# Two transformer blocks on one core: gate one-hots laid out token by token, mapping with one scratch tile, fetched rows asked for earlier, a share of the query weights' low parts on GpSimd

## Chip, core and metric

The kernel runs on one core of a Trainium2 chip. The engines work side by side and wait for one another through semaphores: TensorE (PE; its weight loads are listed as PEld), VectorE (DVE), ScalarE (ACT), GpSimd (POOL) and SyncE (SP), which issues most of the DMA transfers. The metric is the device time of one execution in microseconds. "The profile" is a summary page of one profiled execution, "the trace" what can be asked of that same execution.

## The reference

Two blocks follow each other on 256 tokens of width 2048, all in float32. The part around the change is the retrieval of experts in the first block:

```python
q = (zc @ peer_wq).reshape(PEER_CHUNK, 8, 2, 128)
s1 = einsum('chd,hkd->chk', q[:, :, 0], k1);  s2 = einsum('chd,hkd->chk', q[:, :, 1], k2)
v1, i1 = top_k(s1, 16);  v2, i2 = top_k(s2, 16)
cand = (v1[..., :, None] + v2[..., None, :])          # 16 x 16 sums per head
top_s, top_pos = top_k(cand, 16)
expert = take_along_axis(i1 * 128 + i2, top_pos)      # one of 16384 experts
gate = softmax(top_s)
act = gelu(einsum('chkd,cd->chk', peer_u[expert], zc))
out = einsum('chk,chkd->cd', gate * act, peer_v[expert])
```

Ahead of it stand a pooling mixer and a gated linear recurrence with their projections, behind it an attention block, a convolution and an MLP.

## The kernel before

Weights stream from HBM in pieces of 512 KB, `[128, 8, 128]` float32. The loop over pieces, `p`, sets the order of everything: each round issues the DMAs ahead, makes the piece's operands, issues its eight products on TensorE, and then calls `tick`, which moves the generators on that do the rest (`tasks` at once, `bg` by priority under a budget of estimated costs, the numbers behind `yield`). So the order on each engine is fixed when the program is built, and an engine never overtakes its own queue. A ring of twelve buffers holds the pieces. The pieces of most projections are split in a high part (`wh`, `hi`, by ScalarE) and a low part (`wl`, `lo`, by VectorE), three pieces ahead; `st["share"]` gives so many eighths of a low part to GpSimd. Pieces of the expert matrices `peer_u` and `peer_v` are "plain": they are used as they are (L188), with the 176 tokens of `zn` (or of the gated hidden tiles `hd`, `hb`) as the moving operand.

The first 80 tokens (`SETS`: 64 and 16) get their experts' rows by fetching; for the other 176 all 16384 experts are computed and weighted by a gate matrix. What matters here, in the order of the program:

1. Query pieces (`peer_wq`). `post_wq` makes the scores, `topk_head` finds the best 16 per half and head on VectorE.
2. Pieces of `peer_u` begin. `token_rows` transposes the fetched tokens into `zt` and copies it to all partitions with POOL's DMA queue.
3. `mapping(t)`, for each half of 128 tokens: the softmax of the gates (its exponential is ScalarE's, L642, with a table load ahead of it), and the translation of the winners into expert rows and columns. That is a comparison with an index row, a product and a reduction over 128x2048 elements, for each of two sides (L671, L675, L678). Then TensorE transposes the result (L682 to L684). After the first half, `entries` sends the row numbers and gates to small tiles by POOL's DMAs (L728, L730), and `fetched` starts: three rows of all partitions in flight (L746), each multiplied with `zt` on VectorE (L756).
4. Ahead of `peer_u` step 16 (two pieces each) the loop calls `need(["map0", "map1"])`, so the transposes of the second half stand on TensorE behind the same 256 products in any case.
5. `build_G`: for each group of four tokens a one-hot of the row (A) and a one-hot of the column times the gate (B); A comes from a comparison (L823) and a copy on ScalarE (L824), B from a comparison (L826) and a product with the gate (L827), all `[128, 512]`. TensorE multiplies them token by token (L800), ScalarE keeps the result (L807), and every four groups a DMA writes it to HBM (`Gd`). There are two A/B buffers. Groups are woven between pieces, one `yield` each.
6. Ahead of step 36 the loop calls `need(["G"])` and issues all groups that are left, with no pieces between them: the closing run. Then `load_G` reads the matrices back, and the `peer_v` pieces begin.

A float32 product appears in the trace as two instructions, and as two weight loads.

Of the kernel before, what the change touches and what calls it, by code (L numbers as in the profile page):

```python
# [46 lines left out]
def kernel(ctx: ExitStack, tc: tile.TileContext, a, out, upto=99):  # L47
# [491 lines left out]
    def begin_peer():  # L539
# [21 lines left out]
        st["it4"] = pb.tile([128, 128, 4], BF16, name="it4")  # L561
        pool.tensor_copy(st["it4"], iota_r[:, :, None].to_broadcast([128, 128, 4]))
# [3 lines left out]
        later(normed(), 0)  # L566

# [59 lines left out]
    def mapping(t):  # L627
# [10 lines left out]
        if t == 0:  # L638
            yield from wait("zt")
# [24 lines left out]
        eqs = []  # L664
        for i in range(2):
            if t == 0:
                eq = pb.tile([128, 8, 16, 16], F32, name="eq", tag=f"gs{i}")
            else:
                eq = st["S"][:, i].rearrange("p h a (k b) -> p h (a k) b", k=8)
            eqs.append(eq)  # L670
            dve.tensor_tensor(eq, ab[:, i, :, :, None].to_broadcast([128, 8, 16, 16]),  # L671
                              iota_r[:, None, None, 0:16].to_broadcast([128, 8, 16, 16]), op=ALU.is_equal)
            F = st["F1"] if i == 0 else st["F2"]
            yield 3.2
            dve.tensor_tensor(eq, eq, F[:, t, :, None, :].to_broadcast([128, 8, 16, 16]), op=ALU.mult)  # L675
            yield 2.2
        for i in range(2):
            dve.tensor_reduce(ab[:, i], eqs[i], axis=AX.X, op=ALU.add)  # L678
            yield 2.2
        yield 0.0  # L680
# [4 lines left out]
        if t == 0:  # L685
            entries(ab.rearrange("p i h k -> p i (h k)"), G.rearrange("p h k -> p (h k)"))
# [31 lines left out]
    def entries(ab, G):  # L718
# [4 lines left out]
        st["idx"], st["gat"], st["hid"] = [], [], []  # L723
        for i, (t0, n) in enumerate(SETS):
            x = pb.tile([128, n], U32, name=f"idx{i}")
            g = pb.tile([128, n], F32, name=f"gat{i}")
            for q in range(128 // n):
                pool.dma_start(x[q * n:(q + 1) * n], e[t0:t0 + n, q * n:(q + 1) * n])  # L728
            for q in range(128 // n):
                pool.dma_start(g[q * n:(q + 1) * n], G[t0:t0 + n, q * n:(q + 1) * n])  # L730
            st["idx"].append(x)
            st["gat"].append(g)
            st["hid"].append(pb.tile([128, n], F32, name=f"hid{i}"))
        st["units"] = fetched()

    def fetched():
# [13 lines left out]
        for u in range(3):  # L750
            fetch(u)
        for u, (_, i, s) in enumerate(units):
# [37 lines left out]
    def build_G():  # L790

        pb = st["pb"]
        it4 = st["it4"]
# [23 lines left out]
        for b in range(ND // 4 + 1):  # L817
            if b < ND // 4:
                row, col = (st["T"][:, i, None, 4 * b:4 * b + 4].to_broadcast([128, 128, 4]) for i in range(2))
                gate = st["TG"][:, None, 4 * b:4 * b + 4].to_broadcast([128, 128, 4])  # L820
                A, B = st["oh"][b % 2]
                one = pb.tile([128, 128, 4], BF16, name="om", bufs=2)
                dve.tensor_tensor(one, row, it4, op=ALU.is_equal)  # L823
                act.activation(A, one, AF.Copy)  # L824
                one = pb.tile([128, 128, 4], BF16, name="om", bufs=2)
                dve.tensor_tensor(one, col, it4, op=ALU.is_equal)  # L826
# [42 lines left out]
    def begin_u():  # L869
        ready.add("u0")  # L870

    def begin_hidden():
# [4 lines left out]
        for i in range(2):  # L877
# [3 lines left out]
            one.append([t[:, n + 512 * k:n + 512 * k + 512].rearrange("p (j t) -> p j t", t=4) for k in range(2)])  # L881
# [536 lines left out]
    for p in range(NP):  # L1418
# [108 lines left out]
```

## Time and profile before

| | |
|---|---|
| median of three runs | 3059.46 us (3058.08 to 3060.64) |
| the profiled execution | 3059.16 us |
| its span, from the first to the last instruction | 3057.2 us |
| TensorE busy | 2992.2 us, 98% |
| VectorE busy | 1931.7 us, 63% |
| ScalarE busy | 1053.5 us, 34% |
| GpSimd busy | 337.7 us, 11% |
| mean granted TensorE clock | 0.990 of full speed |

A row of the timeline gives the start, the duration, engine, line, operation, output and inputs; the number behind "x" counts merged instructions, and brackets hold the idle time ahead and what ended it. Matmul ends are modelled, so that the durations of neighbours overlap; their pace is read from starts.

### The profile page before, as it was taken

Reading aid. Unit: us, or ns where it says so; the run is one execution under the profiler, and the core shown is the slowest. Engines: PE = TensorE matmul, PEld = TensorE weight load, DVE = VectorE, ACT = ScalarE, POOL = GpSimd, SP = SyncE. Lnnn points to the kernel's source line nnn. Section 1 sums busy time; section 2 is a strip of 40 time slices with the busy share of each in tenths; the row PEclk is TensorE's granted clock in tenths of the full one; section 3 lists DMA queues with packets and bytes.
Section 4 is the critical chain, followed back from the end, with each engine's and each line's share of the span. In section 5 each row is a group of like instructions: output and inputs, shape, how many; then the busy total and the mean of one; then the engine's idle time right before and its main releaser. Section 6 shows DMA issues by size and latency. Waiting matters only on the chain.

```text
span 3057.2 us, 46147 instructions
## 1 busy us (share of the span) xinstructions
PE 2992.2 (98%) x18156; PEld 2773.8 (91%) x18156; DVE 1931.7 (63%) x3296; ACT 1053.5 (34%) x1642; POOL 337.7 (11%) x307
## 2 busy tenths in 40 slices
PE   9999979999999999999999999999998999999997
PEld 7888969999999999999999888888887888888886
DVE  8868864454444444444452888987658666666767
ACT  7754212220000000000001667657555444444444
POOL 0100020012222222222111100001501000000001
PEclk9999989999999999999999999999999999999998
DMA  7466677779999999999996555565654666665653
GB/s 248 156 187 192 220 220 241 255 282 414 395 395 395 391 390 392 395 397 393 395 359 192 163 176 173 183 196 174 196 189 138 199 183 189 186 187 185 187 186 124
DMA packets 208904, 773.44 MB, mean 253 GB/s; under 512 B 21568, under 2 KB 44416, under 8 KB 187776
## 3 DMA queue, kind: packets, MB, share of 16 engines
q1 hardware_dynamic: 161424, 588.98, 56.3%
q0 software_dynamic: 23984, 169.31, 14.1%
q10 hardware_dynamic: 23280, 12.20, 1.4%
q8 instruction: 144, 2.36, 0.3%
q14 instruction: 72, 0.59, 0.1%
HBM read 755.25 MB, written 13.63 MB: 251 GB/s over the span
## 4 chain that ended last, share of the span: by engine, by line
PE 83%; DVE 1%; ACT 0%; issue 0%
PE mm L188 38%; PE mm L122 28%; PE mm L123 14%; PE g L800 3%; DVE R L1198 0%; DVE z L1213 0%; PE g L778 0%; DVE Y L1461 0%; DVE R L1462 0%; PE s L246 0%; DVE Y L1194 0%; PE g L1113 0%; PE g L1093 0%; PE s L1122 0%; DVE wl L1371 0%
## 5 line engine op out<-in xcount | busy, mean ns | idle before, releaser
L122 PE MATMUL mm<-z,wh 128*128 128x512 f32 x2816 | 1001.3, 399 | 16.1 <-DVE z L1213 9.9
L1360 ACT ACTIVATE wh<-wx 128x1024 fp32r<-128x1024 f32 (+1 forms) x579 | 609.7, 1055 | 698.2 <-PE mm L122 380.9
L1371 DVE TENSOR_TENSOR wl<-wx,wh 128x1024 fp32r<-128x1024 f32 (+1 forms) x579 | 706.3, 1222 | 187.0 <-ACT wh L1360 185.9
L123 PE MATMUL mm<-z,wl 128*128 128x256 f32 x2816 | 789.4, 280 | 5.2 <-DVE wl L1371 5.2
L122 PEld LDWEIGHTS mm<-z,wh 128*128 128x128 f32 x2816 | 530.9, 189 | 141.8 <-issue 8.9
L188 PE MATMUL mm<-zn,wx 128*128 128x176 f32 x4096 | 634.6, 313 | 0.0
L188 PEld LDWEIGHTS mm<-zn,wx 128*128 128x128 f32 x4096 | 620.1, 191 | 0.1
L123 PEld LDWEIGHTS mm<-z,wl 128*128 128x128 f32 x2816 | 533.5, 189 | 7.3 <-DVE wl L1371 7.0
L905 DVE TENSOR_TENSOR R<-R,mm 128x176 f32<-128x176 f32 x256 | 86.1, 336 | 552.7 <-PE mm L188 552.7
L188 PE MATMUL mm<-hb,wx 128*128 128x176 f32 x2560 | 392.4, 313 | 0.0
L188 PEld LDWEIGHTS mm<-hb,wx 128*128 128x128 f32 x2560 | 384.2, 190 | 0.0
L122 PE MATMUL mm<-f,wh 128*128 128x512 f32 x1024 | 364.3, 399 | 0.0
L123 PE MATMUL mm<-f,wl 128*128 128x256 f32 x1024 | 287.6, 281 | 0.0
L122 PEld LDWEIGHTS mm<-f,wh 128*128 128x128 f32 x1024 | 192.4, 188 | 48.1
L188 PE MATMUL mm<-hd,wx 128*128 128x176 f32 x1536 | 235.2, 313 | 0.0
L188 PEld LDWEIGHTS mm<-hd,wx 128*128 128x128 f32 x1536 | 230.5, 190 | 0.0
L855 ACT ACTIVATE hb<-mm 128x176 f32<-128x176 f32 x80 | 25.4, 318 | 593.4 <-PE mm L188 570.5
L123 PEld LDWEIGHTS mm<-f,wl 128*128 128x128 f32 x1024 | 193.4, 189 | 0.0
L746 POOL DMA_INDIRECT ga<-in_peer_u_rows_dram,idx x80 | 107.5, 1343 | 523.6 <-DVE hid L756 430.0
L756 DVE CUSTOM_DVE_ANT_0 ga<-ga 128x2048 f32<-128x2048 f32 x64 | 146.2, 2284 | 10.3 <-DMA ga<-in_peer_u_rows_dram,idx 10.3
L746 POOL DMA_INDIRECT ga<-in_peer_v_rows_dram,idx x80 | 102.2, 1277 | 413.4 <-DVE ga L764 216.6
L764 DVE SCALAR_TENSOR_TENSOR ga<-ga,hid 128x2048 f32<-128x2048 f32 x63 | 147.8, 2345 | 0.0
(377 smaller groups left out, 2678.8 us busy)
## 6 DMA issues: line engine op xcount, KB each, us to landing
wx<-in_peer_u_dram SPq DMA_DIRECT2D x256, 512.0 KB
wx<-in_peer_v_dram SPq DMA_DIRECT2D x256, 512.0 KB
wx<-in_w_in_dram SPq DMA_DIRECT2D x191, 512.0 KB
wx<-in_w_up_dram SPq DMA_DIRECT2D x128, 512.0 KB
wx<-in_w_down_dram SPq DMA_DIRECT2D x128, 512.0 KB
wx<-in_w_out_dram SPq DMA_DIRECT2D x32, 512.0 KB
wx<-in_peer_wq_dram SPq DMA_DIRECT2D x32, 512.0 KB
wx<-in_w_o_dram SPq DMA_DIRECT2D x32, 512.0 KB
```

The lines of the kernel that those rows point to most:

```text
L122: pe.matmul(ps, w[0][:, k], z[:, zk], start=first, stop=False, skip_group_check=True)
L123: pe.matmul(ps[:, 0], w[1][:, k], z[:, zk, 0], start=False, stop=last, skip_group_check=True)
L188: pe.matmul(ps, w[:, k], rhs(half, k), start=k == 0 and (split or half == 0), stop=k == 7 and (split or half == 1), skip_group_check=True)
L746: pool.indirect_dma_start(out=x, out_offset=None, in_=rows, in_offset=bass.IndirectOffsetOnAxis(ap=st["idx"][i][:, s:s + 1], axis=0))
L756: dve.tensor_tensor_reduce(out=x, in0=x, in1=y, scale=1.0, scalar=0.0, op0=ALU.mult, op1=ALU.add, accum_out=h[:, s:s + 1])
L764: dve.scalar_tensor_tensor(y, x, h[:, s:s + 1], y, op0=ALU.mult, op1=ALU.add)
L800: pe.matmul(p[:, t], A[:, :, t], B[:, :, t], start=True, stop=True)
L855: act.activation(hidden(g)[:, i], ps, AF.Gelu_apprx_tanh)
L905: dve.tensor_tensor(R[:, k, NG:], R[:, k, NG:], ps, op=ALU.add)
L1360: act.activation(w[:, i:i + n], x[:, i:i + n], AF.Copy)
L1371: dve.tensor_tensor(w[:, i:i + m], x[:, i:i + m], h[:, i:i + m], op=ALU.subtract)
```

## The change

- The one-hots of a group are laid out `[token, 128]` and no longer `[128, token]`. So the four tokens' operands of L800 each lie together, and the comparison reads one element of `T` repeated 128 times against the index row `it1` repeated four times.
- `mapping` uses one scratch tile for both sides, finishing the first before it begins the second, and no longer waits for `zt`; `entries` is called ahead of the transposes.
- `entries` sends only the row numbers of the first set, then `fetched` starts three fetches, then sends the rest. It waits for `zt` ahead of the first use.
- The loop starts fetching one piece earlier, and takes a row every three pieces, not four, until the gate matrices are complete.
- While the query pieces run, three eighths of each low part go to GpSimd.

```diff
-        st["it4"] = pb.tile([128, 128, 4], BF16, name="it4")
-        pool.tensor_copy(st["it4"], iota_r[:, :, None].to_broadcast([128, 128, 4]))
+        st["it1"] = pb.tile([128, 128], BF16, name="it1")
+        pool.tensor_copy(st["it1"], iota_r)
...
+        st["share"] = 3
...
         yield from acquire("map")
-        if t == 0:
-            yield from wait("zt")
...
-        eqs = []
-        for i in range(2):
+        for i, F in enumerate((st["F1"], st["F2"])):
             if t == 0:
-                eq = pb.tile([128, 8, 16, 16], F32, name="eq", tag=f"gs{i}")
+                eq = pb.tile([128, 8, 16, 16], F32, name="eq", tag="gs0")
...
-        for i in range(2):
-            dve.tensor_reduce(ab[:, i], eqs[i], axis=AX.X, op=ALU.add)
-            yield 2.2
-        yield 0.0
+            dve.tensor_reduce(ab[:, i], eq, axis=AX.X, op=ALU.add)
+            yield 2.3
+        if t == 0:
+            entries(ab.rearrange("p i h k -> p i (h k)"), G.rearrange("p h k -> p (h k)"))
+        for _ in range(3):
+            yield 0.0
...
+        def parts(to, x, i):
+            t0, n = SETS[i]
             for q in range(128 // n):
...
+                pool.dma_start(to[i][q * n:(q + 1) * n], x[t0:t0 + n, q * n:(q + 1) * n])
+
+        parts(st["idx"], e, 0)
+        st["units"] = fetched(parts, e, G)
...
         for u in range(3):
             fetch(u)
+        for i in range(1, len(SETS)):
+            parts(st["idx"], e, i)
+        for i in range(len(SETS)):
+            parts(st["gat"], G, i)
+        yield 1
+        yield from wait("zt")
...
-                pe.matmul(p[:, t], A[:, :, t], B[:, :, t], start=True, stop=True)
+                pe.matmul(p[:, t], A[:, t], B[:, t], start=True, stop=True)
...
-                row, col = (st["T"][:, i, None, 4 * b:4 * b + 4].to_broadcast([128, 128, 4]) for i in range(2))
-                gate = st["TG"][:, None, 4 * b:4 * b + 4].to_broadcast([128, 128, 4])
+                row, col = (st["T"][:, i, 4 * b:4 * b + 4, None].to_broadcast([128, 4, 128]) for i in range(2))
+                gate = st["TG"][:, 4 * b:4 * b + 4, None].to_broadcast([128, 4, 128])
...
     def begin_u():
         ready.add("u0")
+        st["share"] = 0
...
-            st.setdefault("due", p + 1)
-            if st["due"] <= p and next(st["units"], 0) != 0:
-                st["left"] = st.get("left", 2 * NG) - 1
-                st["debt"] += 2.3
+            st.setdefault("due", p)
+            if st["due"] <= p:
+                n = next(st["units"], 0)
+                if n == 1:
+                    first = "left" not in st
+                    st["left"] = st.get("left", 2 * NG + 1) - 1
+                    st["debt"] += 0.0 if first else 2.3
...
-                st["due"] += (st["U1"] - 24 - p) / max(st["left"], 1) if "G" in ready else 4
+                    st["due"] += 6 if first else (st["U1"] - 24 - p) / max(st["left"], 1) if "G" in ready else 3
```

What it moves is shown at three places. The first is VectorE, from the end of the first `mapping` on: before, with all of the top-k (L602 to L620) already ahead of it, and the second `mapping` right behind it.

```order
L661 TENSOR_REDUCE sm<-wk 128x8
L662 RECIPROCAL sm<-sm 128x8
L663 TENSOR_TENSOR wk<-wk,sm 128x128
L671 TENSOR_TENSOR eq<-wk,iota_r 128x2048
L675 TENSOR_TENSOR eq<-eq,wk 128x2048
L671 TENSOR_TENSOR eq<-wk,iota_r 128x2048
L675 TENSOR_TENSOR eq<-eq,wk 128x2048
L678 TENSOR_REDUCE wk<-eq 128x128 x2
L722 SCALAR_TENSOR_TENSOR eidx<-wk 128x128
L641 TENSOR_TENSOR wk<-wk 128x128
```

The same place in the changed kernel, whose lines L660 to L673 are those steps and L621, L603 the merged additions and the first scan of the top-k:

```order
L660 TENSOR_REDUCE sm<-wk 128x8
L661 RECIPROCAL sm<-sm 128x8
L662 TENSOR_TENSOR wk<-wk,sm 128x128
L668 TENSOR_TENSOR eq<-wk,iota_r 128x2048
L671 TENSOR_TENSOR eq<-eq,wk 128x2048
L673 TENSOR_REDUCE wk<-eq 128x128
L668 TENSOR_TENSOR eq<-wk,iota_r 128x2048
L671 TENSOR_TENSOR eq<-eq,wk 128x2048
L673 TENSOR_REDUCE wk<-eq 128x128
L718 SCALAR_TENSOR_TENSOR eidx<-wk 128x128
L621 TENSOR_TENSOR wk<-wk 128x32
```

The first `mapping` has moved ahead of 75 of the program's top-k rows (all of the second half's that were left); its head begins where an L620 of 128x32 stood. Three fetched rows stand among those top-k rows now, and a fourth behind the first long instruction of the second `mapping`; before, one fetched row stood in its middle.

The second place is ScalarE at the second exponential, before (L855 is the activation of a `peer_u` step, L691 and L692 the results of `mapping`):

```order
L855 ACTIVATE hd_3973<-mm 128x176 x5
L691 ACTIVATE T<-s 128x2x48
L692 ACTIVATE TG<-s 128x48
L642 ACT_TABLE_LOAD
L642 ACTIVATE wk<-wk,r_3651 128x128
L855 ACT_TABLE_LOAD
L855 ACTIVATE hd_3973<-mm 128x176
```

And now, with L856, L687, L688 and L641 for the same four:

```order
L687 ACTIVATE T<-s 128x2x48
L688 ACTIVATE TG<-s 128x48
L856 ACTIVATE hd_3994<-mm 128x176 x5
L641 ACT_TABLE_LOAD
L641 ACTIVATE wk<-wk,r_3680 128x128
L856 ACT_TABLE_LOAD
L856 ACTIVATE hd_3994<-mm 128x176
```

The results of the first half have moved ahead of the five activations; the second exponential has stayed between the fifteenth and the sixteenth. The first one has moved from behind the last copy of `zt` (L712) to behind the third.

The third place is TensorE at the end of the gate build, before:

```order
L188 MATMUL mm<-zn,wx 128x176 x16
L800 MATMUL g<-hb_4236,hb_4235 128x128 x4
L188 MATMUL mm<-zn,wx 128x176 x8
L800 MATMUL g<-hb_4236,hb_4235 128x128 x4
L188 MATMUL mm<-zn,wx 128x176 x8
L800 MATMUL g<-hb_4236,hb_4235 128x128 x60
```

And now (L801 is L800's successor):

```order
L188 MATMUL mm<-zn,wx 128x176 x8
L801 MATMUL g<-hb_4271,hb_4270 128x128 x4
L188 MATMUL mm<-zn,wx 128x176 x8
L801 MATMUL g<-hb_4271,hb_4270 128x128 x72
L188 MATMUL mm<-zn,wx 128x176 x80
```

The closing run has grown from 60 products, 15 groups, to 72, 18 groups; 26 of the 44 groups stand between pieces, before it was 29. The transposes of the first half stand 96 products of L188 ahead of those of the second, before 16; those of the second stand behind 256 products as before. On POOL, 29 low parts (128x384) of the query pieces are new.

## Rows read from the trace of the kernel before

**Rows 1.** The page, part 1: busy time, share of the span, instructions.
```profile
PE 2992.2 (98%) x18156; PEld 2773.8 (91%) x18156; DVE 1931.7 (63%) x3296; ACT 1053.5 (34%) x1642; POOL 337.7 (11%) x307
```

**Rows 2.** Waits of TensorE, whole span: us in total, times, longest.
```profile
PE s L682 <- DVE wk L678: 21.1, 1, 21.1
```

**Rows 3.** Timeline of TensorE at the second mapping.
```profile
453.02 0.45 PE L682 MATMUL s<-ident,wk 128*128 128x128 f32 x1 [21.13 <-DVE wk L678]
455.13 0.48 PE L683 MATMUL s<-ident,wk 128*128 128x128 f32 x1 [1.66 <-DVE wk L678]
...
455.61 6.70 PE L188 MATMUL mm<-zn,wx 128*128 128x176 f32 x32
```

**Rows 4.** Windows: five engines' busy us, then granted clock, DMA share, GB/s.
```profile
434.00:436.00 2.00, 0.00 (x0) 0.00 (x0) 0.00 (x0) 0.00 (x0) 0.16 (x1) 0.82 0.97 389
```

**Rows 5.** Timeline of VectorE, top-k and mapping.
```profile
371.75 0.43 DVE L620 TENSOR_TENSOR wk<-wk 128x32 f32<-128x32 f32 x4
...
392.92 0.27 DVE L641 TENSOR_TENSOR wk<-wk 128x128 f32<-128x128 f32 x1
...
405.02 0.29 DVE L661 TENSOR_REDUCE sm<-wk 128x8 f32<-128x128 f32 x1 [9.17 <-ACT wk L642]
...
438.30 2.29 DVE L756 CUSTOM_DVE_ANT_0 ga<-ga 128x2048 f32<-128x2048 f32 x1 [10.35 <-DMA ga<-in_peer_u_rows_dram,idx]
...
440.79 0.28 DVE L661 TENSOR_REDUCE sm<-wk 128x8 f32<-128x128 f32 x1
...
450.60 4.47 DVE L678 TENSOR_REDUCE wk<-S 128x128 f32<-128x2048 f32 x2
```

**Rows 6.** Timeline of ScalarE at a copy of zt and the second exponential.
```profile
374.51 0.59 ACT L712 ACTIVATE ga<-s 64x512 f32<-64x512 f32 x1 [2.51 <-PE s L710]
...
426.83 0.32 ACT L855 ACTIVATE hd<-mm 128x176 f32<-128x176 f32 x1 [4.46 <-PE mm L188]
...
427.52 1.28 ACT L642 ACT_TABLE_LOAD   x1
428.82 0.40 ACT L642 ACTIVATE wk<-wk,r 128x128 f32<-128x128 f32 x1
```

**Rows 7.** The chain that ended last, gate build: start, us, what.
```profile
462.31 1.93 PE g L800 x8
...
609.17 28.32 PE g L800 x120
```

**Rows 8.** Timeline of TensorE in the pieces of peer_u.
```profile
384.30 0.60 PE L710 MATMUL s<-ident,zg 128*16 128x128 f32 x4
384.73 4.94 PE L188 MATMUL mm<-zn,wx 128*128 128x176 f32 x32
389.51 0.60 PE L710 MATMUL s<-ident,zg 128*16 128x128 f32 x4
```

**Rows 9.** Groups by line: busy us, mean ns, idle time before them.
```profile
L1371 DVE TENSOR_TENSOR wl<-wx,wh 128x1024 fp32r<-128x1024 f32 (+1 forms) x579 | 706.3, 1222 | 187.0 <-ACT wh L1360 185.9 <-ACT rs_e L237 0.4
...
L827 DVE TENSOR_TENSOR hb<-om,TG 128x512 f32<-128x512 bf16 x44 | 30.5, 692 | 71.3 <-PE g L800 69.8 <-DVE om L826 1.4
...
L823 DVE TENSOR_TENSOR om<-T,it 128x512 bf16<-128x512 bf16 x44 | 18.6, 423 | 0.9 <-ACT hb L824 0.3
```

**Rows 10.** Timeline of VectorE in the closing run of the gate build.
```profile
611.14 0.69 DVE L827 TENSOR_TENSOR hb<-om,TG 128x512 f32<-128x512 bf16 x1 [0.65 <-PE g L800]
...
613.02 0.69 DVE L827 TENSOR_TENSOR hb<-om,TG 128x512 f32<-128x512 bf16 x1 [0.46 <-PE g L800]
```

**Rows 11.** Windows: query stage, and the stage of peer_u and peer_v.
```profile
290.00:320.00 30.00, 30.00 (x181) 26.53 (x180) 27.11 (x100) 13.15 (x21) 0.00 (x0) 1.00 0.58 175
...
700.00:900.00 200.00, 200.00 (x1342) 200.00 (x1342) 90.16 (x122) 6.36 (x20) 48.58 (x32) 1.00 1.00 399
```

**Rows 12.** Line 1368, POOL's share of a low part: ns min/median/max.
```profile
L1368 POOL TENSOR_TENSOR wl<-wx,wh x3: 917/1257/2282, 2313.8 to 2317.4; 128x256 fp32r<-128x256 f32 x3
```

**Rows 13.** Timeline of VectorE in add_y, beside POOL and just after.
```profile
2303.16 1.48 DVE L1213 SCALAR_TENSOR_TENSOR z<-R,vec,z 128x256 fp32r<-128x256 f32 x1
...
2307.92 0.47 DVE L1213 SCALAR_TENSOR_TENSOR z<-R,vec,z 128x256 fp32r<-128x256 f32 x1
```

More of the change, by code (lines that the diff above doesn't have):

```diff
@@ L684, in mapping @@
         pe.transpose(p[:, 1, :128], G.rearrange("p h k -> p (h k)"), ident)
-        if t == 0:
-            entries(ab.rearrange("p i h k -> p i (h k)"), G.rearrange("p h k -> p (h k)"))
         yield 0.0
@@ L722, in entries, with fetched @@
         dve.scalar_tensor_tensor(e, ab[:, 0], 128.0, ab[:, 1], op0=ALU.mult, op1=ALU.add)
[L723 to L726, printed above, removed]
-            for q in range(128 // n):
[L728 to L736, printed above, removed]
+        st["idx"] = [pb.tile([128, n], U32, name=f"idx{i}") for i, (_, n) in enumerate(SETS)]
+        st["gat"] = [pb.tile([128, n], F32, name=f"gat{i}") for i, (_, n) in enumerate(SETS)]
+        st["hid"] = [pb.tile([128, n], F32, name=f"hid{i}") for i, (_, n) in enumerate(SETS)]
+        def parts(to, x, i):
+            t0, n = SETS[i]
+            for q in range(128 // n):
+                pool.dma_start(to[i][q * n:(q + 1) * n], x[t0:t0 + n, q * n:(q + 1) * n])
+        parts(st["idx"], e, 0)
+        st["units"] = fetched(parts, e, G)
+    def fetched(parts, e, G):
         pb = st["pb"]
@@ L792, in build_G @@
         pb = st["pb"]
-        it4 = st["it4"]
+        it = st["it1"][:, None, :].to_broadcast([128, 4, 128])
         gs = {}
@@ L818, in build_G @@
             if b < ND // 4:
-                row, col = (st["T"][:, i, None, 4 * b:4 * b + 4].to_broadcast([128, 128, 4]) for i in range(2))
-                gate = st["TG"][:, None, 4 * b:4 * b + 4].to_broadcast([128, 128, 4])
+                row, col = (st["T"][:, i, 4 * b:4 * b + 4, None].to_broadcast([128, 4, 128]) for i in range(2))
+                gate = st["TG"][:, 4 * b:4 * b + 4, None].to_broadcast([128, 4, 128])
                 A, B = st["oh"][b % 2]
-                one = pb.tile([128, 128, 4], BF16, name="om", bufs=2)
-                dve.tensor_tensor(one, row, it4, op=ALU.is_equal)
+                one = pb.tile([128, 4, 128], BF16, name="om", bufs=2)
+                dve.tensor_tensor(one, row, it, op=ALU.is_equal)
                 act.activation(A, one, AF.Copy)
-                one = pb.tile([128, 128, 4], BF16, name="om", bufs=2)
-                dve.tensor_tensor(one, col, it4, op=ALU.is_equal)
+                one = pb.tile([128, 4, 128], BF16, name="om", bufs=2)
+                dve.tensor_tensor(one, col, it, op=ALU.is_equal)
                 dve.tensor_tensor(B, one, gate, op=ALU.mult)
@@ L880, in begin_hidden @@
             st["hb"].append(t[:, :n].rearrange("p (a e t) -> p a e t", a=2, e=8))
-            one.append([t[:, n + 512 * k:n + 512 * k + 512].rearrange("p (j t) -> p j t", t=4) for k in range(2)])
+            one.append([t[:, n + 512 * k:n + 512 * k + 512].rearrange("p (t j) -> p t j", t=4) for k in range(2)])
         st["oh"] = list(zip(*one))
@@ L1439 @@
         if "units" in st and plain(p):
[L1440 to L1445 removed]
+            st.setdefault("due", p)
[6 more added lines that the diff above has]
+                    st["due"] += 6 if first else (st["U1"] - 24 - p) / max(st["left"], 1) if "G" in ready else 3
+                elif n == WAIT:
+                    st["due"] += 1
         whole(lo(p + 3))
```

6 lines of the change are left out of this document (2 added, 4 removed).

## The prediction

> **What bounds the kernel now.** I read the page first: TensorE has 2992.2 us of busy time in a span of 3057.2 [rows 1], so a change pays only where TensorE stands still or where its own instructions get shorter. The waits of TensorE come next; the longest is one single wait of 21.1 us, for a reduction of `mapping` on VectorE [rows 2]. The timeline places it: TensorE reaches the transposes of the second token half at 453.02 - 21.13 = 431.89, starts the second of them at 455.13, and then needs 6.70 us for 32 products [rows 3] that take 4.94 us elsewhere [rows 8]. [...]
>
> VectorE's own timeline shows why it is late. The top-k ends at 392.92, and from there it idles 9.17 us for ScalarE's exponential and 10.35 us for the first fetched rows, before the last steps of the second `mapping` run from 440.79 to 450.60 + 4.47 = 455.07 [rows 5].
>
> The second place is the chain that ended last. While the gate matrices are built, each group of four tokens holds TensorE 1.93 us with 8 instructions of L800, 29 groups between weight pieces; then 15 groups run in one stretch of 28.32 us [rows 7]. That is 29 x 1.93 + 28.3 = 84.3 us of TensorE.
>
> **Part one: one-hots contiguous.** L800 takes 1.93 / 8 = 241 ns per instruction. Transposes that also stream 128 float32 columns, but without gaps, go at (384.73 - 384.30) / 4 = 108 ns, and products that load 128 full weight columns without gaps and stream 176 go at (389.51 - 384.73) / 32 = 149 ns [rows 8]. L800 reads both operands with a step of four elements; afterwards both lie together. I take the row with as many streamed columns, 0.108 x 8 = 0.87 us per group; 149 ns would be 1.19, and 1.93 if nothing changes.
>
> VectorE pays something for it. The comparison against the index row takes 423 ns for 512 bfloat16 elements, and the product that follows, with a float32 operand, 692 ns for as many [rows 9]. In the old comparison four neighbours of the token operand lie side by side under the innermost loop; in the new one a single element is repeated 128 times there. No row shows that form, so its cost lies between 0.42 (or a little below) and 0.69 us. [...]
>
> [...]
>
> The order shows 26 groups between pieces and 18 in the closing run. Between pieces TensorE has at least 2.4 us of other work per group, and VectorE's work hides there: 26 x 0.87 = 22.6 us. In the closing run nothing hides it. VectorE's cycle is now 613.02 - 611.14 - 0.46 of waiting = 1.42 us [rows 10]; with two comparisons at 0.69 it becomes 1.42 + 2 x 0.27 = 1.96 us, longer than TensorE's 0.87. The first two groups of the run are ready when TensorE arrives; the third waits for its product (0.69), and 15 more cycles follow: 0.87 + 0.69 + 15 x 1.96 + 0.87 = 31.8 us. Sum 22.6 + 31.8 = 54.4 us against 84.3: **29.9 us less**. The tail itself gets 3.5 us longer and TensorE idles in half of it; if the clock drops there, the next 32 products cost 6.70 - 4.94 = 1.8 us more and the last group 0.9. I take nothing, and keep 2.7 us for the range.
>
> **Part two: mapping without its waits.** On VectorE the first `mapping` now stands where the merged additions stood at 371.75. Its head takes 405.02 - 9.17 - 392.92 = 2.93 us, to 374.7. Its exponential follows the third copy of `zt` on ScalarE: 374.51 + 0.59, a table load of 1.28, the exponential 0.40 [rows 6], so 376.8; another 14.3 us (the length from 440.79 to 455.07) and the index entries stand at about 391. The rest of the top-k is 392.92 - 371.75 = 21.2 us, with three fetched rows in it at 2.29: 419. The second head brings it to 422.
>
> What is late next: the second exponential. ScalarE's order keeps it behind the fifteenth activation of the `u` steps, which ends with a TensorE piece: 426.83 (0.33 later, since three transposes now stand ahead of it) + 0.32 + 1.28 + 0.40 = 429.2 [rows 6]. VectorE idles 7 us there, does the 14.28 us of the old tail and one fetched row of 2.29, and ends at 429.2 + 16.6 = 445.8. TensorE still reaches its transposes at about 431.9, as the order keeps them behind the same products. The second transpose starts at 445.8 and not at 455.13: **9.3 us less**. [...] One scratch tile for two costs nothing: the six long instructions stood one behind another on VectorE anyway. Bounds: 0, if the fetched rows use up more than the slack, and 9.3 + 7 if the exponential were early.
>
> **Part three: rows asked for early.** The first three fetches leave POOL at about 395, and the first is used at about 408; in the old order the first was used 7.7 us after POOL issued it. The eighteen small copies and the `zt` copies queue on POOL behind them, and so does the fourth fetch, but VectorE needs that only after 432. Fetches then come every three pieces, not four. Per 3 pieces and 2 groups, 8.9 us, DMA must bring 1.57 MB of weights, 1.05 MB of rows, and write 0.52 MB of gates: 350 GB/s. Later in the kernel 399 GB/s are carried with TensorE busy for 200.00 of 200 us [rows 11]. I take nothing.
>
> **Part four: POOL's share.** 29 weight pieces of the query product give 3/8 of their low part to POOL. TensorE waits for no low part in this stage (its one long wait is the other), and VectorE's instruction of 1.22 us [rows 9] is ready three pieces ahead. So nothing is gained. The cost is hidden by that lead; without it, it is the second rival below.
>
> **Sum.** 29.9 + 9.3 = 39.2 us. The profiled execution took 3059.16 us (span 3057.2), 0.3 below the median of 3059.46. 3059.2 - 39.2 = **3020 us**.
>
> **Rivals.**
> *The comparison keeps its 0.42 us.* For it: the index operand still lies together. The closing run is then 0.87 + 0.69 + 15 x 1.42 + 0.87 = 23.7 us, and the time 3012.
>
> *POOL and VectorE take turns in the query stage.* VectorE is busy 27.11 of 30 us there while TensorE issues 181 instructions, 18 per piece: 2.98 us a piece, 2.69 of it VectorE's [rows 11]. POOL's form for 256 columns took 917 ns at best and 2282 at worst [rows 12], so 1.4 to 3.4 us for 384. Beside a POOL instruction VectorE's 128x256 took 1.48 us, and 0.47 after it had ended [rows 13]. If every VectorE instruction had to wait for POOL's, a piece would take 2.69 - 0.46 + 1.4 = 3.6 us, 0.65 above TensorE's, over 29 pieces 19 us, less the lead of about 9: 3030. It decides from 2.4 us on POOL: 29 x (2.23 + 2.4 - 2.98) - 9 = 39 eats the whole gain; at 3.4 us the kernel is slower, near 3088. Against it: POOL starts as soon as the high part is there, so a late VectorE finds it done, and this would not pile up.
> [...]
>
> *The early rows come late.* VectorE works in order, so a fetched row that isn't there holds back the top-k. Three waits like the 10.35 us of the first one are 31 us, 7 of them slack: 24 us lost, 3044; one such wait costs 3 us.
>
> *The layout isn't what makes L800 slow.* Then 26 x 1.93 and 18 x 1.96 are 85.5 us, only `mapping` gains, and the time is 3051.
>
> **How the numbers follow.** A measurement of this kernel tells about 0.2%, 6 us, from no change. The forecast has 0.64, the fast comparison 0.13, the turns 0.10 (0.03 of it slower than before), late rows 0.08, the layout 0.04, others 0.01. Faster by more than 6 us: 0.94; within: 0.03; slower: 0.03. The range goes from the fast comparison with a little more from `mapping`, 3010, to the forecast with a cold tail and a mild case of turns or late rows, 3033. The likeliest case alone is 3014 to 3027.
>
> **What would show it.** L800's successor: 8 instructions per 0.87 us between pieces. The closing run: 18 groups in 32 us, TensorE waiting there for the product on VectorE, the comparison near 690 ns. The transposes of the second half: a wait of about 14 us. VectorE: an idle time of some 7 us for the second exponential and none for fetched rows. The stage from 700 to 1600 must look the same. I am wrong if TensorE waits for low parts before 350 us, if the wait for `mapping` stays above 20 us, or if the closing run is shorter than 26 us.

## The result and the profile after

| | before | after |
|---|---|---|
| median | 3060.05 us (3058.08 to 3060.87, 4 runs) | 3026.65 us (3025.21 to 3028.18, 4 runs) |
| span of the profiled execution | 3057.2 us | 3024.2 us |

The ratio is 0.9894, with an interval from 0.9881 to 0.9907: faster by 33.4 us, inside the predicted range, and 6.6 us above the predicted 3020. The page, part 1, after; TensorE's row is 37 us shorter than before [rows 1]:

```profile
PE 2955.1 (98%) x18156; PEld 2734.4 (90%) x18156; DVE 1949.3 (64%) x3296; ACT 1053.5 (35%) x1642; POOL 367.2 (12%) x336
```

The waits of TensorE after (us in total, times, longest), and its timeline at the second mapping. L801 is the old L800, L680 and L681 are the old L682 and L683:

```profile
PE s L680 <- DVE wk L673: 11.6, 1, 11.6
...
PE g L801 <- DVE hb L828: 7.4, 10, 1.0
PE s L681 <- DVE wk L673: 6.3, 1, 6.3
...
PE g L801 <- ACT gst L808: 1.8, 2, 1.3
```

```profile
440.76 0.45 PE L680 MATMUL s<-ident,wk 128*128 128x128 f32 x1 [11.58 <-DVE wk L673]
447.51 0.47 PE L681 MATMUL s<-ident,wk 128*128 128x128 f32 x1 [6.31 <-DVE wk L673]
...
447.99 6.28 PE L188 MATMUL mm<-zn,wx 128*128 128x176 f32 x32
454.11 1.05 PE L801 MATMUL g<-hb,hb 128*128 128x128 f32 x8
455.00 2.55 PE L188 MATMUL mm<-zn,wx 128*128 128x176 f32 x16
```

The long wait [rows 2] is now in two parts, one for each side of the mapping. TensorE arrives at 440.76 - 11.58 = 429.18 and has the second transpose at 447.51: 18.3 us of stall, where it was 455.13 - 431.89 = 23.2 [rows 3]. That is 4.9 us less, not 9.3. VectorE's timeline shows what the rest became (rows answering to [rows 5]):

```profile
426.51 0.29 DVE L660 TENSOR_REDUCE sm<-wk 128x8 f32<-128x128 f32 x1 [6.70 <-ACT wk L641]
...
427.27 2.28 DVE L668 TENSOR_TENSOR S<-wk,iota_r 128x2048 f32<-128x2048 f32 x1
433.79 2.29 DVE L757 CUSTOM_DVE_ANT_0 ga<-ga 128x2048 f32<-128x2048 f32 x1 [4.23 <-DMA ga<-in_peer_u_rows_dram,idx]
...
445.17 2.29 DVE L673 TENSOR_REDUCE wk<-S 128x128 f32<-128x2048 f32 x1
```

The 6.70 us for the second exponential was forecast (7). The 4.23 us for a fetched row, the fourth, was not. POOL's timeline, with the small copies (L726) and the fetches (L741), shows when it was asked for:

```profile
397.14 0.94 POOL L741 DMA_INDIRECT ga<-in_peer_u_rows_dram,idx  x1 [0.30 <-issue]
398.08 2.50 POOL L726 DMA_DIRECT2D idx<-eidx  x5
402.80 0.49 POOL L726 DMA_DIRECT2D idx<-eidx  x1 [2.21 <-DMA ga<-in_peer_u_rows_dram,idx]
406.69 0.48 POOL L726 DMA_DIRECT2D idx<-eidx  x1 [3.40 <-DMA ga<-in_peer_u_rows_dram,idx]
410.51 0.48 POOL L726 DMA_DIRECT2D idx<-eidx  x1 [3.34 <-DMA ga<-in_peer_u_rows_dram,idx]
...
421.22 0.99 POOL L741 DMA_INDIRECT ga<-in_peer_u_rows_dram,idx  x1 [0.30 <-issue]
```

Behind the third fetch five small copies go out, and the next three stand still until one fetch each has landed. So the fourth fetch leaves at 421.22 and is there at 433.79, while VectorE wanted it at 429.56. Of the 23.1 us between the end of the third fetch's issue and the fourth, the 25 copies (18 small ones and 7 of `zt`) take 12.2 us of POOL to issue, and 10.9 us are waits.

The kernel's source does not write these waits; the operand fields of the DMA instructions, which the trace keeps and the timeline leaves out, show where they come from. The built program gives POOL's transfers eight semaphores in turn, 111 to 118 (all 188 in this trace, and in the one before), and a transfer waits until the one that had its number before has landed. The three fetches took 114, 115 and 116 and the five copies 117, 118, 111, 112 and 113; the sixth copy takes 114 again and so waits for the first fetch (2.21 us). These waits are the program's, not the DMA queue's.

In the gate build each group between pieces costs 455.00 - 454.11 = 0.89 us of TensorE. Its timeline in the closing run, first and last rows of the 18 groups:

```profile
568.03 1.05 PE L801 MATMUL g<-hb,hb 128*128 128x128 f32 x8
569.60 2.26 PE L801 MATMUL g<-hb,hb 128*128 128x128 f32 x16 [0.52 <-ACT gst L808]
572.73 1.13 PE L801 MATMUL g<-hb,hb 128*128 128x128 f32 x8 [0.87 <-DVE hb L828]
575.13 1.16 PE L801 MATMUL g<-hb,hb 128*128 128x128 f32 x8 [1.27 <-ACT gst L808]
...
599.10 3.25 PE L801 MATMUL g<-hb,hb 128*128 128x128 f32 x16 [0.30 <-DVE hb L828]
```

It lasts from 568.03 to 602.35, 34.3 us (forecast 31.8). VectorE's timeline there gives its cycle, and the groups by line (busy us, mean ns) the comparison L824, whose predecessor took 423 ns [rows 9]:

```profile
576.01 0.69 DVE L828 TENSOR_TENSOR hb<-om,TG 128x512 f32<-128x512 bf16 x1
576.62 0.68 DVE L824 TENSOR_TENSOR om<-T,it 128x512 bf16<-128x512 bf16 x1
577.22 0.69 DVE L827 TENSOR_TENSOR om<-T,it 128x512 bf16<-128x512 bf16 x1
578.01 0.69 DVE L828 TENSOR_TENSOR hb<-om,TG 128x512 f32<-128x512 bf16 x1
```

```profile
L824 DVE TENSOR_TENSOR om<-T,it 128x512 bf16<-128x512 bf16 x44 | 30.2, 687 | 0.4
```

From product to product it is 578.01 - 576.01 = 2.00 us. The whole build, from TensorE's restart to the end of the last group, took 609.17 + 28.32 - 455.61 = 181.9 us before [rows 3, 7] and 602.35 - 447.99 = 154.4 after: 27.5 us less.

Two differences are not the change's. After the same stall of 2.1 us near 134 us, where both kernels still issue the same instructions, the granted clock fell in the execution before and not in the one after; the first row of each fence shows it, in TensorE's windows (busy us, instructions, granted clock, DMA share, GB/s), before and after:

```profile
130.00:140.00 10.00, 7.89 (x34) 0.83 0.29 81
...
210.00:220.00 10.00, 10.00 (x59) 1.00 0.64 201
...
2320.00:2322.00 2.00, 1.07 (x6) 1.00 0.98 395
```

```profile
130.00:140.00 10.00, 7.82 (x42) 1.00 0.25 81
...
210.00:220.00 10.00, 10.00 (x60) 1.00 0.62 182
...
2288.00:2290.00 2.00, 2.00 (x7) 0.50 0.00 0
```

By the second mapping the execution after is 431.89 - 429.18 = 2.7 us ahead. The clock is less than half of that: by 157 us the lead is 0.85 us. The other 1.86 us come between 160 and 257 us, where TensorE is busy throughout at the full clock in both and yet goes through the same products 1.9% faster after; the second rows show a stretch of it. Four of the fourteen profiled executions have this faster pace (after, joined, pace, step_weights), one of them with the low clock near 134 us too, and it lies almost wholly ahead of GpSimd's first share at 252 us; what makes it was not followed. Behind the gate build the execution after loses 3024.2 - 602.35 - (3057.2 - 637.49) = 2.1 us, with equal work. The last rows belong to 1.6 us of it: at the start of the MLP TensorE stands still twice, and after the second time the clock fell to half in the execution after, not in the one before. So the spans' 33.0 us are 4.9 + 27.5 + 2.7 - 2.1.

### The profile page after: what moved, and what is told of

The parts are those of the page before. It is cut to its first block, busy times and chain, and to the rows that moved or that the text cites. A ratio compares the mean times of both kernels' runs of the same rounds, so it can differ in the third digit from the quotient of the medians.

```text
span 3024.2 us, 46238 instructions
## 1 busy us (share of the span) xinstructions
PE 2955.1 (98%) x18156; PEld 2734.4 (90%) x18156; DVE 1949.3 (64%) x3296; ACT 1053.5 (35%) x1642; POOL 367.2 (12%) x336
## 4 chain that ended last, share of the span: by engine, by line
PE 94%; DVE 3%; DMA 1%; ACT 1%; issue 0%; POOL 0%; SPq 0%; DVEq 0%; POOLq 0%; ACTq 0%
PE mm L188 39%; PE mm L122 35%; PE mm L123 18%; PE g L801 1%; DMA ga<-in_peer_u_rows_dram,idx 1%; DVE wl L1373 0%; DVE wk L673 0%; DVE hb L828 0%; DMA idx<-eidx 0%; DVE R L1200 0%; PE s L586 0%; PE s L396 0%; DVE z L1215 0%; PE g L779 0%; DVE Y L1468 0%
## 5 line engine op out<-in xcount | busy, mean ns | idle before, releaser
L1373 DVE TENSOR_TENSOR wl<-wx,wh 128x1024 fp32r<-128x1024 f32 (+2 forms) x579 | 696.5, 1206 | 189.0 <-ACT wh L1362 186.5
L188 PE MATMUL mm<-zn,wx 128*128 128x176 f32 x4096 | 633.2, 313 | 0.0
L188 PEld LDWEIGHTS mm<-zn,wx 128*128 128x128 f32 x4096 | 616.2, 190 | 0.1
L188 PE MATMUL mm<-hb,wx 128*128 128x176 f32 x2560 | 392.4, 313 | 0.0
L188 PEld LDWEIGHTS mm<-hb,wx 128*128 128x128 f32 x2560 | 384.2, 190 | 0.0
L188 PE MATMUL mm<-hd,wx 128*128 128x176 f32 x1536 | 235.2, 313 | 0.0
L188 PEld LDWEIGHTS mm<-hd,wx 128*128 128x128 f32 x1536 | 230.5, 190 | 0.0
L856 ACT ACTIVATE hb<-mm 128x176 f32<-128x176 f32 x80 | 25.4, 317 | 582.7 <-PE mm L188 582.7
L741 POOL DMA_INDIRECT ga<-in_peer_u_rows_dram,idx x80 | 100.1, 1251 | 493.3 <-DVE hid L757 427.3
L741 POOL DMA_INDIRECT ga<-in_peer_v_rows_dram,idx x80 | 101.9, 1274 | 433.1 <-DVE ga L765 255.6
```

What stands on the lines that cost most here:

```text
L188: pe.matmul(ps, w[:, k], rhs(half, k), start=k == 0 and (split or half == 0), stop=k == 7 and (split or half == 1), skip_group_check=True)
L741: pool.indirect_dma_start(out=x, out_offset=None, in_=rows, in_offset=bass.IndirectOffsetOnAxis(ap=st["idx"][i][:, s:s + 1], axis=0))
L856: act.activation(hidden(g)[:, i], ps, AF.Gelu_apprx_tanh)
L1373: dve.tensor_tensor(w[:, i:i + m], x[:, i:i + m], h[:, i:i + m], op=ALU.subtract)
```

## Experiments

All medians stand beside runs of the kernel before on the same chip, whose medians lay between 3058.48 and 3059.34 us; differences to the changed kernel are taken from its 3026.65.

The theory: the layout gives some 27 us, the mapping 5, POOL's share nothing; the mapping's missing part is the fourth row behind POOL's copies, and the closing run has VectorE's pace. Rivals: the layout needs the other parts; the share brought the 2.7 us; the row is slow whenever it is asked for.

### The layout alone

```diff
 # the kernel before
-st["it4"] = pb.tile([128, 128, 4], BF16, name="it4")
+st["it1"] = pb.tile([128, 128], BF16, name="it1")
-pe.matmul(p[:, t], A[:, :, t], B[:, :, t], start=True, stop=True)
+pe.matmul(p[:, t], A[:, t], B[:, t], start=True, stop=True)
...
```

> The kernel before with the one-hots laid together and nothing else. Theory: the layout brings most of the gain, 26 or more groups at 0.89 us in place of 1.93 and a closing run at about 2.0 us per group: with the 29 and 15 groups of the old order 29 x 0.89 + 15 x 2.0 = 56 us against 84, so 28 us less, about 3031. Rival: TensorE's gain needs the other parts too (the pieces wait for VectorE between groups): 3045 or more.

Measured 3032.05 us (3030.32 to 3033.89), ratio 0.9914 [0.9897, 0.9930]: 26.7 us of the 33, close to the theory, far from the rival.

### POOL's share taken out, and the share alone

```diff
 # the changed kernel (first run); the kernel before with the opposite sign (second)
-st["share"] = 3
```

> The changed kernel without POOL's 3/8 of the low parts in the query stage. Theory: nothing hangs on it, and the 2.7 us by which the changed kernel was ahead before 360 us are the clock after an early stall, which differs between executions: 3026.6 as it stands, within 1.5 us, and the head of the first mapping within 3 us of 365.7. Rival: the freed VectorE is what brings TensorE earlier to the mapping: about 2.7 us slower, 3029.

> The kernel before with POOL's 3/8 of the low parts in the query stage and nothing else. Theory: nothing hangs on it; 3059 within 2 us, the same time as before, and TensorE reaches the second mapping's transposes at the same distance from the start of the query stage. Rival: VectorE freed of 3/8 of these parts brings the top-k, and with it the mapping that TensorE waits for, earlier by 2 us or more: 3057 or less.

Taken out: 3028.91 us (3027.16 to 3033.80), 2.3 more, beyond the 1.5 that the theory allowed but with ranges that overlap; its profiled execution had the low clock near 134 us (0.83) and not the faster pace behind it. That alone left the question open. The share alone settles it: 3058.50 against 3058.48, ratio 1.0005 [0.9996, 1.0014], with TensorE's wait for the mapping at 20.80 us (21.1 before). The windows from 240 to 330 us (busy us of TensorE, its weight loads, VectorE, ScalarE and POOL), before and with the share alone, show why: TensorE is busy for all 90 us in both, so there is no wait for VectorE to shorten.

```profile
240.00:330.00 90.00, 90.00 (x530) 79.13 (x529) 77.07 (x231) 43.09 (x64) 0.00 (x0) 1.00 0.59 187
```

```profile
240.00:330.00 90.00, 90.00 (x529) 79.08 (x528) 75.87 (x235) 42.64 (x63) 32.67 (x26) 1.00 0.59 188
```

VectorE's part of a piece takes 826 ns in the median instead of 1.22 us, but its busy time in this stretch fell by 1.2 us alone. The groups by line in this window say why: the low parts take 5.9 us less (30.6 for 36.5), although those of 640 columns have a mean of 941 ns with 803 at the least, while VectorE's two products that make `zn` and `zg`, the same 32 instructions, take 15.9 us in place of 11.0 (513 and 480 ns each in place of 394 and 295). The scans of the top-k, with one tensor each, kept their times (MAX8 280 ns, 283 before). So these instructions, each with two input tensors, do slow down beside GpSimd, and nothing waits for them here; what slows them no run shows.

### Rows asked for as before, and the copies sent first

```diff
 # old_rows: fetched() and its calls (one row every four pieces) as in the kernel before
+yield from wait("zt")
 for u in range(3):
     fetch(u)
-yield from wait("zt")
...
 # copies_first: all eighteen small copies in entries(), ahead of the fetches
+for i in range(len(SETS)):
+    parts(st["idx"], e, i)
+for i in range(len(SETS)):
+    parts(st["gat"], G, i)
```

> The changed kernel with the fetched rows asked for as before: all small copies first, fetches only once zt is there, one row every four pieces. Theory: asking early gained nothing by itself; without it only three rows lie ahead of the second mapping's end, and 16 groups instead of 18 stand in the closing run: the second transposes come up to 6.5 us earlier (no fourth row and no wait for it) and the closing run is 2 us cheaper: 3018 to 3022. Rival: without asking early the first row is again waited for some 10 us, more than the 6.7 us that VectorE idles for the second exponential, and holds back the top-k and the mapping: 3027 to 3030.

> The changed kernel with all eighteen small copies issued ahead of the first three fetches. Theory: the fourth fetched row was late (4.23 us of VectorE's idle time in the second mapping) because it queued on POOL behind copies that themselves waited for the three fetches; now it leaves POOL near 411 and VectorE finds it there, so the second transposes start 4 us earlier: 3022.5. The first row may wait up to 5 us, which the idle time before the second exponential takes up. Rival: the row is late because its transfer is slow beside the weights (12.5 us from issue to landing) or waits for the zt copies: nothing gained, 3026.6.

The old order of the rows: 3027.52 us (3027.02 to 3028.24), 0.9 more than with the early rows. VectorE waits 14.89 us for the first row:

```profile
417.70 2.29 DVE L753 CUSTOM_DVE_ANT_0 ga<-ga 128x2048 f32<-128x2048 f32 x1 [14.89 <-DMA ga<-in_peer_u_rows_dram,idx]
```

The second transpose stands 451.44 - 367.65 = 83.8 us behind the candidates of the top-k that come last before 375 us, against 447.51 - 365.67 = 81.8. Asking early so gained 2.0 us there and gave them back in the gate build, which takes 154.4 us instead of 602.65 + 1.13 - 451.92 = 151.9, with 18 groups instead of 16 in the closing run because of it. The 0.9 us between the medians is not resolved. The time lies in the rival's range, and its long wait for the first row is there.

Copies first: 3025.45 us (3023.01 to 3026.41), 1.2 less, not resolved by time alone. POOL's and VectorE's timelines, this kernel (here L744 is the fetch, L756 its use, L711 a copy of `zt`):

```profile
415.61 0.48 POOL L711 DMA_DIRECT2D zt<-zt  x1 [3.37 <-DMA ga<-in_peer_u_rows_dram,idx]
421.62 2.38 POOL L744 DMA_INDIRECT ga<-in_peer_u_rows_dram,idx  x1 [5.53 <-DMA ga<-in_peer_u_rows_dram,idx]
```

```profile
411.64 2.29 DVE L756 CUSTOM_DVE_ANT_0 ga<-ga 128x2048 f32<-128x2048 f32 x1 [3.19 <-DMA ga<-in_peer_u_rows_dram,idx]
...
433.38 2.29 DVE L756 CUSTOM_DVE_ANT_0 ga<-ga 128x2048 f32<-128x2048 f32 x1 [0.99 <-DMA ga<-in_peer_u_rows_dram,idx]
```

The fourth fetch did not leave at 411: two copies of `zt`, now first in line behind the fetches, stood still for them in the same way, and then the fetch itself, whose turn had the third fetch's semaphore (118), for 5.53 us. The wait for the fourth row fell to 0.99 us and the first row's 3.19 went into VectorE's idle time, so the second transpose came at 447.11 - 368.50 = 78.6 us behind the same row, 3.2 earlier. In both kernels the sixth place behind the fetches is the first to be held, by a small copy (2.21 us) as by one of `zt` (2.08). The theory had the cause right, a wait behind the fetches, and the remedy wrong.

### An earlier exponential

```diff
-tick(2.1 if plain(p) else 1.25)
+tick((2.4 if "zn" in ready and "map1" not in ready else 2.1) if plain(p) else 1.25)
```

> The changed kernel with the planner's budget per piece at 2.4 instead of 2.1 between the norm and the end of the second mapping, so that top-k and head of the mapping stand earlier in the order of every engine: the second exponential then stands on ScalarE behind the twelfth activation instead of the fifteenth, and on VectorE two fetched rows stand in the second mapping's tail, the fourth behind its end. Theory: what is left of TensorE's wait is 6.70 us for the exponential, 4.23 us for the fourth row and 2.29 us of work on it; without them the tail ends near 437 instead of 447.46 and the time falls by about 10 us: 3016.5. Rival one: the exponential, now early, waits for VectorE itself and holds back the activations behind it, TensorE waits for their buffers, and half or more is lost: 3021 or more. Rival two: the rows, late beside the weights, hold VectorE in any order: 3022 or more.

Measured 3014.78 us (2999.71 to 3016.43), ratio 0.9838 [0.9811, 0.9864]: 11.9 less, near the theory. TensorE's and VectorE's timelines:

```profile
433.34 0.33 PE L681 MATMUL s<-ident,wk 128*128 128x128 f32 x1 [1.67 <-DVE wk L673]
...
442.74 2.04 PE L801 MATMUL g<-hb,hb 128*128 128x128 f32 x8 [4.19 <-DVE hb L828]
```

```profile
414.56 0.28 DVE L660 TENSOR_REDUCE sm<-wk 128x8 f32<-128x128 f32 x1 [0.69 <-ACT wk L641]
...
438.30 2.29 DVE L757 CUSTOM_DVE_ANT_0 ga<-ga 128x2048 f32<-128x2048 f32 x1 [5.02 <-DMA ga<-in_peer_u_rows_dram,idx]
```

Of the 18.3 us of stall 1.67 are left. The fourth row is late still, now behind the mapping, where the first one-hots queue behind it and TensorE waits 4.19 us.

### The old comparison, one-hots together

```diff
-one = pb.tile([128, 4, 128], BF16, name="om", bufs=2)
+one = pb.tile([128, 128, 4], BF16, name="om", bufs=2)
-act.activation(A, one, AF.Copy)
+act.activation(A, one.rearrange("p j t -> p t j"), AF.Copy)
...
```

> The changed kernel with the comparisons in their old layout (four neighbours of the token operand under the innermost loop, 0.42 us before) and the one-hots still written together: ScalarE's copy and VectorE's product read the comparison's result with a step of four. Theory: the closing run goes at VectorE's pace, 2.00 us per group with two comparisons at 0.69; at 0.42 it goes at about 1.46, 18 groups take 9 us less, and nothing changes between the pieces: 3017.5. If the low clock there, at which TensorE takes about 1.8 us per group, then sets the pace, 4 us less: 3022.5. Rival: the product or the copy get slower by the step and eat it: 3026 or more.

Measured 3018.01 us, ratio 0.9867 [0.9851, 0.9884]: 8.6 less, as the theory had it, with the low clock absent from this closing run (granted clock 1.00 from 560 to 620 us). The comparison's group, and TensorE in the closing run, which now waits for ScalarE's copies (L808 and L825):

```profile
L824 DVE TENSOR_TENSOR om<-T,it 128x512 bf16<-128x512 bf16 x44 | 18.5, 421 | 0.7 <-ACT hb L825 0.2
```

```profile
579.80 1.16 PE L801 MATMUL g<-hb,hb 128*128 128x128 f32 x8 [0.50 <-ACT gst L808]
581.18 1.16 PE L801 MATMUL g<-hb,hb 128*128 128x128 f32 x8 [0.23 <-ACT gst L808]
582.65 1.16 PE L801 MATMUL g<-hb,hb 128*128 128x128 f32 x8 [0.30 <-ACT gst L808]
```

### More groups between pieces

```diff
-st["debt"] += 0.0 if first else 2.3
+st["debt"] += 0.0 if first else 1.2 if "map1" in ready and "G" not in ready else 2.3
```

> The changed kernel with the planner's cost of a fetched row at 1.2 instead of 2.3 while the gates are built, so that 38 groups stand between pieces and 6 in the closing run, instead of 26 and 18. Theory: between pieces a group costs TensorE 0.89 us, in the closing run about 1.95; twelve groups moved are 12 x 1.06 = 13 us less, VectorE having 3.26 us a piece for 2.00 + 2.29 / 3 = 2.76: 3014. Rival: VectorE, now nearly full, or the transfers (weights, rows and gates at 350 GB/s or more) make TensorE wait between the pieces, and half or more is lost: 3020 or more.

Measured 3012.79 us (3008.60 to 3016.94), ratio 0.9852 [0.9836, 0.9868]: 13.9 less. TensorE is busy for the whole stretch from 460 to 560 us, and the six groups of the closing run start at 577.64 and end near 586.9.

### The three together, and the copies parted by need

```diff
 # joined: the three edits above; joined_rows: these two as well
 parts(st["idx"], e, 0)
+for i in range(len(SETS)):
+    parts(st["gat"], G, i)
...
+if 8 <= u < 16:
+    n = SETS[1][1]
+    t0, q = SETS[1][0], u - 8
+    pool.dma_start(st["idx"][1][q * n:(q + 1) * n], e[t0:t0 + n, q * n:(q + 1) * n])
+    if q:
+        pool.dma_start(st["zt"][1][q * n:(q + 1) * n], st["zt"][1][:n])
```

> The three edits early exponential, old comparison with the one-hots still together, and 38 groups between pieces, in one kernel. Theory: they act in different stretches except the last two: from 3014.8 the comparison takes 18 x 0.5 = 9 us off the closing run, and the twelve groups moved between pieces now save 12 x (1.46 - 0.89) = 7 us instead of 13: 2999. The wait of 5.02 us for the fourth row, behind which the first one-hots queue on VectorE and TensorE for 4.19, is still there. Rival: the gains overlap more (both closing-run edits pay for the same idle time of TensorE): 3005 or more.

> The same, with the small copies parted by need: the gate values (ten) ahead of the first fetches, the index rows and the copies of the second set's input (fifteen) spread over the ninth to the sixteenth fetched row. Theory: the fourth fetch no longer queues behind copies that wait for the fetches, leaves POOL near 412 instead of 421 and is there when VectorE comes to it; TensorE's wait for the first one-hots, 4.19 us, and the low clock after it fall away: 4 to 5 us less than the kernel without this edit, 2995. Rival: the transfer beside the weights takes its 12 us whenever it is asked, or later rows are delayed by the spread copies: no gain.

The three together: 2995.66 us, 3.3 under the theory, ratio 0.9780 [0.9755, 0.9805]. With the copies parted: 2992.55 us, ratio 0.9789 [0.9773, 0.9805]. Their medians are 3.1 us apart and their ranges (2979.99 to 2998.25; 2991.79 to 2995.27) overlap, and the ratios do not part them either, so the step between them is read from the trace. POOL, VectorE and TensorE with the copies parted (L762 is the use of a row, L806 the groups):

```profile
410.10 0.96 POOL L744 DMA_INDIRECT ga<-in_peer_u_rows_dram,idx  x1 [8.18 <-DVE wk L640]
```

```profile
432.00 2.28 DVE L762 CUSTOM_DVE_ANT_0 ga<-ga 128x2048 f32<-128x2048 f32 x1
```

```profile
432.14 0.33 PE L681 MATMUL s<-ident,wk 128*128 128x128 f32 x1 [1.67 <-DVE wk L673]
...
437.19 1.05 PE L806 MATMUL g<-hb,hb 128*128 128x128 f32 x8
440.47 1.05 PE L806 MATMUL g<-hb,hb 128*128 128x128 f32 x8
```

The fourth fetch leaves at 410.10, where it was 422.84 in the three together; its turn's semaphore is free, and it waits only until VectorE has finished with the first row and so freed a buffer. VectorE finds the row there. The second group starts 440.47 - 432.14 = 8.3 us behind the second transpose; without this edit it is 444.06 - 431.41 = 12.7. So its place behind the copies made the row late: asked for in time it was there in time. How long its transfer took in this run is not shown, since nothing waited for it; in the changed kernel it was 433.79 - 421.22 = 12.6 us.

### Which operand's step costs

```diff
 # step_weights: A with a step of four, B together; step_stream: the other way round
-pe.matmul(p[:, t], A[:, t], B[:, t], start=True, stop=True)
+pe.matmul(p[:, t], A[:, :, t], B[:, t], start=True, stop=True)
...
```

> The changed kernel with the one-hot that is loaded as weights (A) laid out with a step of four elements again, the streamed one (B) together. The trace of before has, per group, 241 ns for each of 8 instructions with both operands stepped, 111 ns afterwards; which operand cost it is open. If the load of the weights is the cost: 1.93 us per group as before, 26 groups between pieces 27 us more, the closing run nearly as now, since VectorE sets its pace at 2.0: 3053. If it is the streamed operand: 0.89 us and 3026. If each gives its share: between, 1.4 us per group and 3040.

> The changed kernel with the streamed one-hot (B) laid out with a step of four elements again, the one loaded as weights (A) together. If the streamed operand is the cost: 1.93 us per group and 3053. If the load of the weights is: 0.89 us and 3026. If each gives its share: 1.4 us and 3040. If both operands must be stepped for the cost to show, or either is enough, this run and the one with A stepped agree.

Measured 3053.50 us, ratio 0.9981 [0.9971, 0.9992], and 3057.73 us, ratio 0.9997 [0.9986, 1.0008]. TensorE's timelines, A stepped, then B stepped:

```profile
501.07 1.99 PE L801 MATMUL g<-hb,hb 128*128 128x128 f32 x8
502.90 4.94 PE L188 MATMUL mm<-zn,wx 128*128 128x176 f32 x32
```

```profile
500.79 1.97 PE L801 MATMUL g<-hb,hb 128*128 128x128 f32 x8
502.59 2.57 PE L188 MATMUL mm<-zn,wx 128*128 128x176 f32 x16
```

1.83 and 1.80 us per group: one stepped operand, either of them, costs nearly all that both did (1.93). That is the last case of the second expectation, either is enough. In these two kernels the writer of the stepped tile was slower as well (ScalarE's copy 1140 ns instead of 629, VectorE's product 1089 instead of 692), which weighs in the closing run but not on TensorE's instructions.

## Why the prediction was right, and where its sizes were off

**Part one, one-hots.** Right as a mechanism: 0.89 us per group between pieces against 0.87, the comparison at 0.69, VectorE as the pace of the closing run. The 0.69 us was the author's estimate, as no row had the new form; it took 687 ns for 512 elements, as long as the product with a float32 operand (692), against 423 in the old form [rows 9]. What makes the new form slower no run shows. The term was 29.9 us and measured 27.5: the closing run took 34.3 us instead of 31.8, since VectorE's cycle is 2.00 us and not 1.96 (0.6 us over 15 cycles), and two groups wait 0.52 and 1.27 us for ScalarE's copy of an earlier result, which the sum did not have. The clock fell in the closing run as feared (0.85 from 570 to 604, and 0.50 at its lowest), and cost nothing: a group then takes TensorE some 1.8 us (1.81 at 586.98), still under VectorE's 2.00. The 2.7 us kept for a cold tail were an estimate from the stall of the kernel before, where the clock had fallen [rows 4], to 0.50 from 436 to 455, and was 0.70 in the mean over the next 7 us: 1.8 for the products behind the tail [rows 3, 8] and 0.9 for its last group. Neither came: the last group takes 602.19 - 601.22 = 0.97 us, and the 66 products behind it 10.01 / 66 = 152 ns each, where the kernel before has 6.70 / 32 = 209 behind the stall and 4.94 / 32 = 154 elsewhere. The rival with the fast comparison was wrong for this kernel, but its price, 8 us, was right: the run with the old comparison gained 8.6.

**Part two, mapping.** 9.3 us forecast, 4.9 measured. The second exponential came as worked out (6.70 us of idle time). What failed is the sentence under part three that the small copies queue ahead of the fourth fetch "but VectorE needs that only after 432". VectorE wanted it at 429.56, 432.3 with the 2.7 us added back by which this execution was ahead, so that half was right; but the sum never worked out when the row comes. It gave the copies no time on POOL, while their issue took 12.2 us and three of them waited 2.21, 3.40 and 3.34 us for the fetches ahead, whose semaphores they had to take over. Without the waits the fetch would have left near 410 and, at 12.6 us of transfer, been there near 423 (an estimate from these rows); with them it came 4.23 us late. That is the mild case of the rival "the early rows come late". Its price of 3 us is near by luck: it was worked out for a wait of 10.35 us ahead of 7 us of slack, and this one is shorter and has no slack behind it.

**Part three, early rows.** "Cost nothing" holds only in sum: 2.0 us gained in the mapping, about as much lost in the gate build, and 0.9 us between the medians, which is not resolved. The transfers were no limit: TensorE was busy throughout between pieces (100 of 100 us from 460 to 560) at 338 to 350 GB/s.

**Part four, POOL's share.** Nothing gained and nothing lost, as forecast; the share alone gave a ratio of 1.0005. Of the rival "POOL and VectorE take turns" the slowing is there, in `zn`, `zg` and the low parts (`zg` 480 ns in place of 295), but TensorE stayed busy (90.00 of 90 us), so that it cost no time.

The sum: 39.2 us forecast; of the 33.0 in the spans 32.4 are the change (27.5 + 4.9), and 0.6 are what is left of the two differences between the executions (2.7 - 2.1). The 6.8 us missing are 2.4 of part one and 4.4 of part two.

## What to carry to other kernels

When a wait is taken away, work out the arrival of everything that stands in the waiting engine's order up to the place that sets the end, rows fetched by another queue included: one transfer that was never late before can take over the wait. Where such a transfer waits for one it doesn't need, look at the semaphores in the trace before blaming the queue: here eight of them went round, and the ninth transfer waited for the first. Put what is needed late behind, and not between. And when TensorE's own instructions get shorter, look at the engine that feeds them and at where the work stands: the same group cost 0.89 us of TensorE's time between pieces and 1.9 in a run of its own, so a planner's cost, one number, was worth 14 us, and the comparison's form 9.

## What the runs showed of the hardware

- With a step of four float32 elements (16 bytes) in either operand of a product, the loaded or the streamed one, an instruction took 225 to 241 ns instead of 111 ns (225 with the streamed one stepped, 229 with the loaded one, 241 with both). What makes the step slow no run shows.
- VectorE's two products that make `zn` and `zg`, with two input tensors each, took up to 1.6 times as long, in the mean, with GpSimd's subtractions beside them (`zn` 513 ns in place of 394, `zg` 480 in place of 295, the share alone against before); its scans with one tensor did not change (MAX8 280 ns, 283 before).
- After one and the same stall of 2.1 us the granted clock fell in some executions (0.83 from 130 to 140 us, before) and stayed in others (1.00, after), worth some 0.9 us; and at the full clock the same products ran at two paces, 347 or 353 ns a pair between 160 and 257 us, worth 1.9 us. A difference of 3 us between two single executions need not be the kernel's: on one chip those of the kernel before lay between 3046.81 and 3064.58 us.
